# Experts of 56 slots with gathers for four pairs, gates by comparison, and a delta-net convolution that reads PSUM

## The chip, the cores and the metric

One program runs on one core of a Trainium2 chip. The metric is the device time of one execution in microseconds (us). A core has five engines that run side by side, each with its own instruction queue: TensorE (PE, matrix products, with a separate path PEld that loads the stationary operand), VectorE (DVE), ScalarE (ACT), GpSimd (POOL), and SyncE (SP), which here issues the DMAs. TensorE writes its results to PSUM, eight banks of 512 float32 columns on 128 partitions; everything else lies in SBUF.

## The reference

The input is 512 tokens of 1024 features. A first block has two layers (forgetting attention, then retention, each with a memory attention beside it). The second block has one layer: a mixer (a short convolution path and a gated delta net), then a mixture of experts, then a norm. The change touches the second block only. In short:

```
qkv  = silu(causal_dwconv(concat(q, k, v), conv_w))        # four taps along the tokens
q    = q * rsqrt(sum(q*q) + eps) * 128**-0.5 ; k likewise  # per head and token
y_a  = rms_norm(b * causal_dwconv(c * h, conv_a_w))        # three taps
...
group = argmax(h @ router_group_w)                         # 4 groups
two experts of the group's 8 by softmax, gate = group_prob * p / sum(p)
out[token] += gate * (silu(x @ w_gate[e]) * (x @ w_up[e])) @ w_down[e]
```

There are 32 experts and 512 x 2 = 1024 assignments of tokens to experts. Each expert has three float32 matrices of 2 MiB. With the inputs that are timed, the reference's router gives an expert between 19 and 41 assignments.

## The kernel before

Products in full float32 precision are made from two rounded halves (`wh`/`wl` of a weight, `hH`/`hL` of an activation), three products each, accumulated in an `acc` bank; four `acc` banks go round.

**Mixer.** `dn` walks a fixed list of pieces, `DN_ORDER`: f (a delta-net head's projections, convolutions and triangular inverse, up to the first yield of `dn_head`), s (the same head's scan over four chunks of tokens), z (an output gate), a (a quarter of the short convolution). The order of instructions on each engine inside this is chosen by the framework's scheduler, from dependencies and its own costs; PE then executes its queue strictly in that order. A projection is 24 matmuls into one `acc` bank. `conv` (L1186) handles its result: ACT copies the bank to a padded tile `cpad` (L1259), DVE scales it by the first tap (L1195) and adds three shifted taps (L1197) into `cy`. ACT makes tanh (L1261), DVE the silu `cs` (L1263), PE transposes `cs`, ACT squares the result (L1271), DVE sums the squares (L1272), and a reciprocal root of them scales Kh or Qh. The `acc` bank is free when ACT's copy is done.

**Experts.** Expert `e` owns 64 slots (`CAP`). `route` finds for each assignment its slot number `dest`; `build_S` (L1656, L1657) makes a 0/1 matrix `S3` of tokens by slots; `gather_T` multiplies the token features (`xH` and `xL`, L230 through `mm`) by it, which gives `mhT`, features by slots. One such gather serves a "quad": two pairs of experts, 4 x 64 = 256 slots, 64 matmuls of 256 columns. Experts are taken in 16 pairs. Per pair: `gate_up` of expert 0 and 1 (64 rows each, gate and up side by side, `pg`), `gu_out` (ACT scales by the slot's gate `us`), `act_T` (four PE transposes, then tanh and two DVE steps into `h`), `down` (`pd`), `y_out` (splits `pd` into `yh`, `yl`) and, a pair later, `combine` (16 matmuls with the 0/1 matrices `ST`, results added to `x` by DVE, L1852). `gates` (L1744 to L1755) gets `us` by four small matmuls of `gxs` with `S3` and eight tiny DVE steps. In this part PE's order is the order in which the code is written (`self.pe = self.ordered(...)`); DVE's and ACT's is the scheduler's.

**Weights.** Each expert's matrices come as six tiles of 1 MiB (1.0486 MB), in order of use, through a ring of 12 + 6 = 18 buffers (`wtile`, `NWA` + `NWB`). SP issues the DMA of a tile (L1767, L1812) when the matmuls that read the buffer's last content are done. 32 experts make 192 tiles.

Assignments beyond an expert's slots would go through `overflow`, a loop whose count comes from `spill`; with at most 41 to an expert it runs zero times.

Of the kernel before, what the change touches and what calls it, by code (L numbers as in the profile page):

```python
# [35 lines left out]
CAP = 64  # L36
NPAIR = NE // 2
SLOTS = NE * CAP
MAXOV = 16
# [3 lines left out]
NWB = 6  # L43
# [11 lines left out]
CM = ["ones", "iota", "ustrict", "eend", "pcol"]  # L55
# [8 lines left out]
def constants():  # L64
# [4 lines left out]
    c["ones"] = np.ones((P, P))  # L69
# [23 lines left out]
    c["pcol"] = np.stack([i, (i + CAP) % P], 1) - P  # L93
# [30 lines left out]
class Model:  # L124
# [689 lines left out]
    def out_router(self, W, heads):  # L814
# [13 lines left out]
        cm = self.rtp.tile([P, sum(self.off[k][1] for k in CM)], F32, tag="cm", name="cm")  # L828
        nc.sync.dma_start(cm, A["cm"])
        iota = self.const(cm, "iota")  # L830
        self.io3 = rp.tile([P, 2, CAP], F32, tag="io3", name="io3")
        V.tensor_copy(self.io3.rearrange("p a n -> p (a n)"), iota)
# [4 lines left out]
        V.tensor_copy(self.onesb, self.const(cm, "ones"))  # L837
        V.tensor_copy(self.ustb, self.const(cm, "ustrict"))
        V.tensor_copy(self.eend, self.const(cm, "eend"))
        V.tensor_scalar(out=self.e64b, in0=self.eend[0:1, :], scalar1=float(-CAP), scalar2=None, op0=ALU.add)  # L840
        self.pcol = rp.tile([P, 2, NPAIR], F32, tag="pcol", name="pcol")
        ends = self.eend.rearrange("p (n e) -> p n e", e=2)[:, None, :NPAIR, 1]
        nc.gpsimd.tensor_tensor(self.pcol, ends.to_broadcast([P, 2, NPAIR]),
                                self.const(cm, "pcol")[:, :, None].to_broadcast([P, 2, NPAIR]), op=ALU.add)
# [341 lines left out]
    def conv(self, wk, src, width, wv):  # L1186

        nc = self.nc
        V = nc.vector
        pad = width - 1  # L1190
        cp = wk.tile([P, S + 3], F32, tag="cpad", bufs=1, name="cpad")
        V.memset(cp[:, :pad], 0.0)
        src(cp[:, pad:pad + S])
        y = wk.tile([P, S], F32, tag="cy", name="cy")
        V.tensor_scalar(out=y, in0=cp[:, 0:S], scalar1=wv(0), scalar2=None, op0=ALU.mult)  # L1195
        for j in range(1, width):
            V.scalar_tensor_tensor(out=y, in0=cp[:, j:j + S], scalar=wv(j), in1=y, op0=ALU.mult, op1=ALU.add)  # L1197
        return y

    def short_conv(self, wk, ct, Wr, C):  # L1200
# [3 lines left out]
        for i in (2, 0, 1):  # L1204
# [4 lines left out]
        y = self.conv(wk, lambda d: V.tensor_tensor(d, pss[1], c, op=ALU.mult), 3,  # L1209
                      lambda j: aw[:, j * 4 + ct:j * 4 + ct + 1])  # L1210
# [18 lines left out]
    def dn_head(self, wk, h, Wr, C, sc, pre):  # L1229
# [23 lines left out]
        for n, (nm, c0) in enumerate(DNC):  # L1253
# [5 lines left out]
            y = self.conv(wk, lambda d: SC.activation(d, ps, AF.Copy), 4, lambda j: cw[:, j * 12 + ci:j * 12 + ci + 1])  # L1259
# [11 lines left out]
            SC.activation(sq, v4(pt), AF.Square)  # L1271
            V.tensor_reduce(ss[:, n * NT:(n + 1) * NT], sq, axis=AX.X, op=ALU.add)  # L1272
# [142 lines left out]
    def moe(self, psd):  # L1415
# [9 lines left out]
        io3 = self.io3  # L1425
        et = mc.tile([P, NPAIR, 1], F32, tag="et", name="et")
        blks = []
        quads = [dict(base=float(q * 2 * P), io=io3, n=2 * P) for q in range(NPAIR // 2)]
        for p in range(NPAIR):
            w = {}  # L1430
            for j in range(2):
                for n, src in (("g", "w_gate_2"), ("u", "w_up_2"), ("d", "w_down_2")):
                    w[n, j] = A[src][0, 2 * p + j]
            nc.gpsimd.tensor_scalar(out=et[:, p, :], in0=self.hm64[:, 1:2], scalar1=float(2 * p), scalar2=None, op0=ALU.add)
            blks.append(dict(pair=p, quad=quads[p // 2], cols=slice(p % 2 * P, (p % 2 + 1) * P), w=w, n=2,
                             e=et[:, p, :], cut=p == NPAIR - 1))
# [10 lines left out]
        self.gather_T(quads[0], True)  # L1447
# [3 lines left out]
        for p in range(nb):  # L1451
            more = p + 1 < nb

            def sums():
                if p:
                    self.combine(blks[p - 1], [(t, n) for n in range(2) for t in range(NT)])
                self.slots(blks[p])
                if more and p % 2:
                    self.build_S(quads[p // 2 + 1])
                if not p:  # L1460
                    ov.extend(self.spill(mc))
# [10 lines left out]
            if more:  # L1472
                if not p:
                    self.act_T(blks[0], 0)
                if p % 2:
                    self.gather_T(quads[p // 2 + 1])
                self.gates(blks[p + 1])
                self.down(blks[p], 0)
                self.act_T(blks[p], 1)
# [15 lines left out]
        self.overflow(mc, wk, io3, gb, ot, *ov)  # L1495

    def route(self, mc):
# [30 lines left out]
        iota = self.io3[:, 0, :]  # L1528
# [66 lines left out]
        G.tensor_tensor(self.gxs[:, :, 4:8], gx, self.gxs[:, :, 0:4].bitcast(F32), op=ALU.subtract)  # L1595

    def spill(self, mc):
# [11 lines left out]
        for m in range(2, 8):  # L1609
# [8 lines left out]
        for i in range(MAXOV):  # L1618
            cmp = sc[:, (8 + i % 2) * NE:(9 + i % 2) * NE]
# [18 lines left out]
    def build_S(self, blk):  # L1638
# [3 lines left out]
        S3 = wk.tile([P, NT, 2 * P], F32R, tag="S3", name="S3")  # L1642
        iof = blk["io"].rearrange("p a n -> p (a n)")
        ds = []
        for n in range(blk["n"] // P):
            dest = blk["dest"]
            if n or not isinstance(blk["base"], float) or blk["base"]:
                db = wk.tile([P, 2 * NT], F32, tag=f"db{n}", name="db")
                V.tensor_scalar(out=db, in0=dest, scalar1=blk["base"] + n * P if n else blk["base"], scalar2=None,
                                op0=ALU.subtract)  # L1650
                dest = db
            ds.append(dest)
        for t in range(NT):
# [7 lines left out]
    def gather_T(self, blk, first=False):  # L1661
# [4 lines left out]
        hT = blk["hT"] = wk.tile([P, KD, 2 * P], F32, tag="mhT", name="mhT")  # L1666
        pss = {}

        def mms(k, t, start):
            if k // 2 not in pss:  # L1670
                pss[k // 2] = self.att()
            o = pss[k // 2][:, k % 2 * 2 * P:k % 2 * 2 * P + n]
            for c, part in enumerate(self.xs):
                self.mm(o, part[:, t, k, :], S3[:, t, :n], start and c == 0,
                        t == NT - 1 and c == 1 and (not first or k % 2 == 1))

        def put(b):
            pv = pss[b].rearrange("p (k n) -> p k n", k=2)[:, :, :n]
            o = hT[:, 2 * b:2 * b + 2, :n]
            if b % 2:  # L1680
                nc.vector.tensor_tensor(o, pv, self.gv[:, 2 * b:2 * b + 2, None].to_broadcast([P, 2, n]), op=ALU.mult)
            else:
                for k in range(2):
                    nc.scalar.activation(o[:, k, :], pv[:, k, :], AF.Copy, scale=self.gv[:, 2 * b + k:2 * b + k + 1])

        if first:
            for t in range(NT):
                for k in range(KD):
                    mms(k, t, t == 0 and k % 2 == 0)
                    if t == NT - 1 and k % 2:  # L1690
                        put(k // 2)
        else:
            for k in range(KD):
                for t in range(NT):
                    mms(k, t, t == 0)
                if k % 2:
                    put(k // 2)
# [286 lines left out]
```

## Time and profile before

| | us |
|---|---|
| median of 3 runs | 1773.61 (1772.92 to 1774.19) |
| the profiled execution | 1773.5 |
| its span in the profile | 1771.7 |
| PE busy | 1724.4 (97%) |
| DVE busy | 1007.2 (57%) |
| ACT busy | 590.6 (33%) |

In the span the mixer takes about 965 to 1206 us, its output projection with the router until about 1251, the experts' loop from 1258 to about 1748, and the final norm the rest. An engine's busy time says how full it is; whether it sets the pace is read from what it waits for.

### The profile page before, as it was taken

Reading aid. Unit: us, or ns where it says so; the run is one execution under the profiler, and the core shown is the slowest. Engines: PE = TensorE matmul, PEld = TensorE weight load, DVE = VectorE, ACT = ScalarE, POOL = GpSimd, SP = SyncE. Lnnn points to the kernel's source line nnn. Section 1 sums busy time; section 2 is a strip of 40 time slices with the busy share of each in tenths; the row PEclk is TensorE's granted clock in tenths of the full one; section 3 lists DMA queues with packets and bytes.
Section 4 is the critical chain, followed back from the end, with each engine's and each line's share of the span. In section 5 each row is a group of like instructions: output and inputs, shape, how many; then the busy total and the mean of one; then the engine's idle time right before and its main releaser. Section 6 shows DMA issues by size and latency. Waiting matters only on the chain.

```text
span 1771.7 us, 24714 instructions
## 1 busy us (share of the span) xinstructions
PE 1724.4 (97%) x9410; PEld 1255.9 (71%) x9410; DVE 1007.2 (57%) x2660; ACT 590.6 (33%) x1173; POOL 96.6 (5%) x143
## 2 busy tenths in 40 slices
PE   8999999999999999999999999999999999999996
PEld 7888888878888888888888777778644445354443
DVE  7655564563757555454657978875545435453534
ACT  7643333433536232222446433334211111111112
POOL 0000000000000110111011000010200000000001
PEclk9999999999999999999999999999999999999998
DMA  8633233233223322223213342326799999999981
GB/s 260 175 96 90 81 93 95 73 86 96 69 92 99 92 85 82 84 75 103 76 48 81 91 111 62 85 69 265 301 418 418 410 409 420 407 407 407 420 321 49
DMA packets 199276, 318.82 MB, mean 180 GB/s; under 512 B 18789, under 2 KB 159590, under 8 KB 174450
## 3 DMA queue, kind: packets, MB, share of 16 engines
q1 hardware_dynamic: 199154, 317.21, 50.6%
q8 instruction: 75, 1.23, 0.3%
q14 instruction: 47, 0.39, 0.1%
HBM read 312.16 MB, written 5.01 MB: 179 GB/s over the span
## 4 chain that ended last, share of the span: by engine, by line
PE 89%; DVE 6%; ACT 2%; DMA 2%; issue 1%; SPq 0%; POOL 0%; POOLq 0%; ACTq 0%; DVEq 0%
PE acc L143 50%; PE pg L230 13%; PE att L143 8%; PE att L230 7%; PE pd L230 6%; PE trp L148 3%; PE trp L230 1%; PE trp L143 1%; DVE wl L205 1%; ACT wh L204 1%; DMA raw<-in_w_mem_kv_dram 1%; DVE cy L1197 1%; PE att L148 0%; ACT hH L243 0%; DMA kvf<-kvd 0%
## 5 line engine op out<-in xcount | busy, mean ns | idle before, releaser
L205 DVE TENSOR_TENSOR wl<-raw,wh 128x1024 fp32r<-128x1024 f32 x184 | 225.8, 1227 | 189.8 <-ACT wh L204 179.8
L143 PE MATMUL acc<-hH,wh 128*128 128x512 f32 (+1 forms) x760 | 297.3, 392 | 5.4 <-DVE sz L578 3.1
L143 PE MATMUL acc<-hL,wh 128*128 128x512 f32 (+1 forms) x760 | 299.1, 394 | 0.0
L143 PE MATMUL acc<-hH,wl 128*128 128x512 f32 (+1 forms) x760 | 298.0, 392 | 0.0
L204 ACT ACTIVATE wh<-raw 128x1024 fp32r<-128x1024 f32 x184 | 194.6, 1059 | 276.8 <-PE acc L143 262.2
L230 PE MATMUL pg<-mw,mhT 128*64 128x512 f32 x1024 | 230.3, 597 | 0.0
L143 PEld LDWEIGHTS acc<-hH,wh 128*128 128x128 f32 x760 | 143.7, 190 | 31.4 <-DVE sz L578 3.3
L143 PEld LDWEIGHTS acc<-hL,wh 128*128 128x128 f32 x760 | 144.0, 189 | 25.4
L143 PEld LDWEIGHTS acc<-hH,wl 128*128 128x128 f32 x760 | 144.0, 189 | 25.4 <-issue 1.0
L230 PEld LDWEIGHTS pg<-mw,mhT 128*64 128x64 f32 x1024 | 69.3, 137 | 129.8 <-issue 129.6
L143 PE MATMUL acc<-wh,hL 128*128 128x256 f32 (+1 forms) x384 | 129.5, 338 | 0.4 <-DVE hL L247 0.4
L143 PE MATMUL acc<-wh,hH 128*128 128x256 f32 (+1 forms) x384 | 129.3, 337 | 0.1
L143 PE MATMUL acc<-wl,hH 128*128 128x256 f32 (+1 forms) x384 | 129.3, 337 | 0.0
L143 PE MATMUL acc<-wh,oh 128*128 128x512 f32 x320 | 127.1, 397 | 1.4 <-ACT oh L243 1.4
L143 PE MATMUL acc<-wl,oh 128*128 128x512 f32 x320 | 126.4, 395 | 0.0
L143 PE MATMUL acc<-wh,ol 128*128 128x512 f32 x320 | 126.2, 395 | 0.0
L230 PE MATMUL pd<-mw,h 128*64 128x512 f32 (+1 forms) x544 | 116.7, 571 | 3.0 <-DVE h L1803 3.0
L1784 ACT ACTIVATE gu<-pg,gt 128x512 f32<-128x512 f32 x32 | 22.0, 687 | 266.7 <-PE pg L230 252.9
L1843 DVE TENSOR_TENSOR yl<-pd,yh 128x512 fp32r<-128x512 f32 x30 | 19.3, 687 | 137.0 <-ACT yh L1842 137.0
L1852 DVE TENSOR_TENSOR x<-att,x 128x512 f32<-128x512 f32 x120 | 73.1, 683 | 31.6 <-PE att L230 31.6
L230 PEld LDWEIGHTS pd<-mw,h 128*64 128x64 f32 x544 | 37.4, 137 | 66.3 <-issue 60.9
L143 PEld LDWEIGHTS acc<-wh,hH 128*128 128x128 f32 x384 | 73.0, 190 | 8.3 <-ACT hH L243 0.8
(567 smaller groups left out, 2863.3 us busy)
## 6 DMA issues: line engine op xcount, KB each, us to landing
mw<-in_w_gate_dram SPq DMA_DIRECT2D x64, 1024.0 KB
mw<-in_w_up_dram SPq DMA_DIRECT2D x64, 1024.0 KB
mw<-in_w_down_dram SPq DMA_DIRECT2D x62, 1024.0 KB
raw<-in_fox_w_in_dram SPq DMA_DIRECT2D x56, 512.0 KB
raw<-in_w_out_dram SPq DMA_DIRECT2D x40, 512.0 KB
raw<-in_w_in_dram SPq DMA_DIRECT2D x28, 512.0 KB
raw<-in_ret_w_in_dram SPq DMA_DIRECT2D x20, 512.0 KB
raw<-in_w_mem_kv_dram SPq DMA_DIRECT2D x16, 512.0 KB
```

The costliest lines, as they stand in the source:

```text
L143: self.pe.matmul(o, l, r, start=start, stop=stop)
L148: self.pe.transpose(o, i, self.ident[b:b + n, b:b + n])
L204: nc.scalar.activation(h, raw, AF.Copy)
L205: nc.vector.tensor_tensor(l, raw, h.bitcast(F32), op=ALU.subtract)
L230: ins = getattr(eng, name)(*a, **k)
L1197: V.scalar_tensor_tensor(out=y, in0=cp[:, j:j + S], scalar=wv(j), in1=y, op0=ALU.mult, op1=ALU.add)
L1784: nc.scalar.activation(gu, pg.rearrange("p (n k) -> p k n", k=4), AF.Copy, scale=blk["us"][:, j:j + 1])
L1843: V.tensor_tensor(l, pd, h.bitcast(F32), op=ALU.subtract)
L1852: self.nc.vector.tensor_tensor(xv, ps, xv, op=ALU.add)
```

## The change

1. `CAP` goes from 64 to 56. A gather then serves four pairs ("oct"): 8 x 56 = 448 slots, 64 matmuls of 448 columns, four gathers in all where there were eight. The halves of 64 rows stay (`RT`): an expert reads 64 columns of `mhT`, its 56 and 8 of a neighbour, whose gate is zero.
2. `mhT` and `S3` grow for that, and the ring of weight tiles goes from 18 to 16 (`NWB` 6 to 4).
3. `gates` compares the slots' numbers with the token rows `rows` on DVE, multiplies by the token's gate `grow` and sums along the tokens, four steps of 512 columns per pair; PE's four matmuls go. `grow` is made once, in `slot_rows`, by 16 matmuls of half width.
4. `conv` starts with ACT's scaled copy of the last tap into `cy`; DVE adds three taps straight from the `acc` bank. `cpad`, the DVE scaling and the memset go.
5. The squares are summed by ACT, four pieces of 128 columns with an accumulator, in place of one piece of 512 and DVE's reduction.
6. Some constants come by DMA in place of copies; `spill` is called after the first `down`.

```diff
-CAP = 64
+CAP = 56
+RT = 64
+OCT = 8 * CAP
...
-NWB = 6
+NWB = 4
...
-    def conv(self, wk, src, width, wv):
+    def conv(self, wk, x, width, wv):
...
-        cp = wk.tile([P, S + 3], F32, tag="cpad", bufs=1, name="cpad")
-        V.memset(cp[:, :pad], 0.0)
-        src(cp[:, pad:pad + S])
         y = wk.tile([P, S], F32, tag="cy", name="cy")
-        V.tensor_scalar(out=y, in0=cp[:, 0:S], scalar1=wv(0), scalar2=None, op0=ALU.mult)
-        for j in range(1, width):
-            V.scalar_tensor_tensor(out=y, in0=cp[:, j:j + S], scalar=wv(j), in1=y, op0=ALU.mult, op1=ALU.add)
+        nc.scalar.activation(y, x, AF.Copy, scale=wv(width - 1))
+        for d in range(1, width):
+            nc.vector.scalar_tensor_tensor(out=y[:, d:], in0=x[:, :S - d], scalar=wv(width - 1 - d), in1=y[:, d:],
+                                           op0=ALU.mult, op1=ALU.add)
...
-            y = self.conv(wk, lambda d: SC.activation(d, ps, AF.Copy), 4, lambda j: cw[:, j * 12 + ci:j * 12 + ci + 1])
+            y = self.conv(wk, ps, 4, lambda j: cw[:, j * 12 + ci:j * 12 + ci + 1])
...
-            SC.activation(sq, v4(pt), AF.Square)
-            V.tensor_reduce(ss[:, n * NT:(n + 1) * NT], sq, axis=AX.X, op=ALU.add)
+            for t in range(NT):
+                SC.activation(sq[:, t, :], v4(pt)[:, t, :], AF.Square, accum_out=ss[:, n * NT + t:n * NT + t + 1])
...
-        quads = [dict(base=float(q * 2 * P), io=io3, n=2 * P) for q in range(NPAIR // 2)]
+        octs = [dict(base=float(q * OCT), n=OCT) for q in range(NPAIR // 4)]
...
-                if more and p % 2:
-                    self.build_S(quads[p // 2 + 1])
-                if not p:
-                    ov.extend(self.spill(mc))
+                if more and p % 4 == 3:
+                    self.build_S(octs[p // 4 + 1])
...
-                if p % 2:
-                    self.gather_T(quads[p // 2 + 1])
+                if p % 4 == 3:
+                    self.gather_T(octs[p // 4 + 1])
...
+        self.grow = self.wk.tile([P, 2, S], F32, tag="grow", name="grow")
+        for i in range(2):
+            ps = self.att()
+            for t in range(NT):
+                for h in range(2):
+                    self.mm(ps[h * RT:(h + 1) * RT, t * P:(t + 1) * P],
+                            self.gr[:, t, i, h:h + 1].to_broadcast([P, RT]), self.ident, True, True)
+            self.nc.scalar.activation(self.grow[:, i, :], ps, AF.Copy)
...
     def gates(self, blk):
+        wk, V = self.wk, self.nc.vector
+        a = wk.tile([P, 2, 2], F32, tag="ga", bufs=2, name="ga")
+        for j in range(2):
+            for i in range(2):
+                junk = wk.tile([P, S], BF16, tag="gj", name="gj")
+                V.scalar_tensor_tensor(out=junk, in0=self.rows[:, i, :], scalar=self.ucol[:, j, blk["pair"]:blk["pair"] + 1],
+                                       in1=self.grow[:, i, :], op0=ALU.is_equal, op1=ALU.mult,
+                                       accum_out=a[:, i, j:j + 1])
+        us = wk.tile([P, 2], F32, tag="us", bufs=2, name="us")
+        V.tensor_tensor(us, a[:, 0, :], a[:, 1, :], op=ALU.add)
...
-                    self.mm(pg[i * CAP:(i + 1) * CAP, :], hT[:, kk, j * CAP:(j + 1) * CAP], wt[i][:, k, :],
+                    self.mm(pg[i * RT:(i + 1) * RT, :], hT[:, kk, c:c + RT], wt[i][:, k, :],
```

How the change moves instructions is seen at three places. First PE, from the end of the first gather (`att<-S`) into the first pair's `gate_up` (`pg`); `dest` and `gr` are the slot and gate columns that `slot_rows` spreads, `gxs` the old gates' operand, `ohb` belongs to `spill`. Before, then now:

```order
L230 MATMUL att<-S_12027,xL 128x256
L230 MATMUL att<-ident,dest 128x128 x8
L230 MATMUL pg<-mw,mhT 64x512 x16
L230 MATMUL trp<-gxs,S_12027 128x8 x4
L230 MATMUL pg<-mw,mhT 64x512 x8
L230 LDWEIGHTS rt
L230 MATMUL att<-ohb,rt 128x32
```

```order
L236 MATMUL att<-S_11985,xL 128x448
L236 MATMUL att<-ident,dest 128x128 x8
L236 MATMUL att<-ident,gr 64x128 x16
L236 MATMUL pg<-mw,mhT 64x512 x32
L236 MATMUL trp<-ident,gu 128x128 x4
L236 MATMUL pd_12278<-mw,h_12263 64x512
L236 MATMUL pd_12279<-mw,h_12263 64x512
```

The two short groups of `gxs` and `ohb` leave the middle of `pg`, 16 half-wide matmuls of `gr` stand in front of it, and `pd` follows `pg` with only the transposes between.

Second DVE, at the same time: the rows that stand just in front of the first pair's two `h` steps, on which the first `pd` waits (`S` is the 0/1 matrix of the next gather, `gj` a gate step, `ebt` part of `spill`). Before, then now:

```order
L1633 TENSOR_TENSOR sc<-sc 128x256
L1621 TENSOR_REDUCE ebt<-sc 128x1 x2
L1635 TENSOR_REDUCE dest_12320<-sc 128x8
L1620 TENSOR_SCALAR sc<-sc 128x32 x2
L1802 SCALAR_TENSOR_TENSOR h_12341<-h_12341,trp 128x256
L1621 TENSOR_REDUCE ebt<-sc 128x1 x2
L1803 SCALAR_TENSOR_TENSOR h_12341<-h_12341,trp 128x256
```

```order
L1663 TENSOR_SCALAR S_12785<-ioh,db 128x224
L1749 SCALAR_TENSOR_TENSOR gj,ga<-rows,pcol,grow 128x512
L1664 SCALAR_TENSOR_TENSOR S_12785<-ioh,db,S_12785 128x224
L1749 SCALAR_TENSOR_TENSOR gj,ga<-rows,pcol,grow 128x512
L1663 TENSOR_SCALAR S_12785<-ioh,db 128x224
L1749 SCALAR_TENSOR_TENSOR gj,ga<-rows,pcol,grow 128x512
L1664 SCALAR_TENSOR_TENSOR S_12785<-ioh,db,S_12785 128x224
L1753 TENSOR_TENSOR us<-ga 128x2
L1749 SCALAR_TENSOR_TENSOR gj,ga<-rows,pcol,grow 128x512
L1822 SCALAR_TENSOR_TENSOR h_12263<-h_12263,trp 128x256
L1749 SCALAR_TENSOR_TENSOR gj,ga<-rows,pcol,grow 128x512
L1823 SCALAR_TENSOR_TENSOR h_12263<-h_12263,trp 128x256
```

Before, small steps of `spill` stand there; now gate steps of the first four pairs and the next `S` do, 16 `gj` rows ahead of the first `h` in all.

Third DVE, at the start of the mixer: the convolution of the first head's k and the steps around it (`wl` is the low half of the next weight). Before, then now:

```order
L205 TENSOR_TENSOR wl<-raw,wh 128x1024
L1195 TENSOR_SCALAR cy<-cpad,vecs 128x512
L1197 SCALAR_TENSOR_TENSOR cy<-cpad,vecs,cy 128x512
L205 TENSOR_TENSOR wl<-raw,wh 128x1024
L1100 TENSOR_SCALAR beta<-beta 128x16
L1102 TENSOR_TENSOR sx<-trp,dtb 128x16
L1101 TENSOR_SCALAR hb<-beta 128x16
L1197 SCALAR_TENSOR_TENSOR cy<-cpad,vecs,cy 128x512
```

```order
L211 TENSOR_TENSOR wl<-raw,wh 128x1024
L1201 SCALAR_TENSOR_TENSOR cy<-acc,vecs,cy 128x511
L211 TENSOR_TENSOR wl<-raw,wh 128x1024
L1201 SCALAR_TENSOR_TENSOR cy<-acc,vecs,cy 128x510
L1109 TENSOR_SCALAR beta<-beta 128x16
L1111 TENSOR_TENSOR sx<-trp,dtb 128x16
L1110 TENSOR_SCALAR hb<-beta 128x16
L1201 SCALAR_TENSOR_TENSOR cy<-acc,vecs,cy 128x509
```

The scaling of `cpad` is gone, and the three taps that are left read the `acc` bank itself.

## Rows read from the trace of the kernel before

**Rows 1.** The page: busy us of the engines; GB/s in 40 slices of the span.

```profile
PE 1724.4 (97%) x9410; PEld 1255.9 (71%) x9410; DVE 1007.2 (57%) x2660; ACT 590.6 (33%) x1173; POOL 96.6 (5%) x143
GB/s 260 175 96 90 81 93 95 73 86 96 69 92 99 92 85 82 84 75 103 76 48 81 91 111 62 85 69 265 301 418 418 410 409 420 407 407 407 420 321 49
```

**Rows 2.** Chain of waits: start us, us, engine and line, instructions.

```profile
1224.46 14.18 PE acc L143 x62
...
1311.50 7.74 PE att L230 x64
1319.24 0.34 PE trp L230 x4
...
1345.93 0.54 PE trp L230 x4
...
1372.82 7.74 PE att L230 x64
...
1744.39 3.60 PE pd L230 x32
```

**Rows 3.** Waits of PE, 1290 to 1715: us in total, times, longest.

```profile
PEld att L230 <- DVE ST L1716: 5.7, 7, 0.8
```

**Rows 4.** Waits of the DMA queue on SP, 1190 to 1771: likewise.

```profile
SPq L1767 <- PE pg L230: 245.5, 55, 22.6
```

**Rows 5.** Stretches: busy us (x) of PE, PEld, DVE, ACT, POOL; PEclk, DMA, GB/s.

```profile
1320.00:1330.00 10.00, 10.00 (x50) 3.48 (x48) 2.40 (x13) 0.38 (x1) 0.00 (x0) 1.00 0.99 392
...
1360.00:1370.00 10.00, 10.00 (x46) 4.78 (x44) 6.08 (x11) 1.36 (x3) 0.00 (x0) 1.00 1.02 423
```

**Rows 6.** Timeline of PE at the loop's start: start us, us, what.

```profile
1258.02 0.36 PE L230 MATMUL att<-S,xH 128*128 128x256 f32 x1 [0.53 <-DVE S L1657]
...
1265.63 1.95 PE L230 MATMUL att<-ident,dest 128*128 128x128 f32 x16
1267.51 7.09 PE L230 MATMUL pg<-mw,mhT 128*64 128x512 f32 x32
...
1285.09 3.65 PE L230 MATMUL pd<-mw,h 128*64 128x512 f32 x16 [1.66 <-DVE h L1803]
```

**Rows 7.** Groups by form, 1300 to 1700: busy us, mean ns, idle before.

```profile
L1716 DVE SCALAR_TENSOR_TENSOR ST<-rows,pcol,ST 128x512 fp32r<-128x512 uint16 x26 | 18.4, 752 | 0.0
L1657 DVE SCALAR_TENSOR_TENSOR S<-io,db,S 128x128 fp32r<-128x128 f32 x48 | 15.2, 346 | 0.1
L1656 DVE TENSOR_SCALAR S<-io,db 128x128 fp32r<-128x128 f32 x48 | 12.3, 280 | 0.0
L1715 DVE TENSOR_SCALAR ST<-rows,pcol 128x512 fp32r<-128x512 uint16 x26 | 11.4, 482 | 0.0
L1803 DVE SCALAR_TENSOR_TENSOR h<-h,trp 128x256 f32<-128x256 f32 x26 | 10.9, 420 | 0.8
```

**Rows 8.** Groups by form in the mixer, 965 to 1206.

```profile
L1197 DVE SCALAR_TENSOR_TENSOR cy<-cpad,vecs,cy 128x512 f32<-128x512 f32 x44 | 32.7, 744 | 0.2
L1195 DVE TENSOR_SCALAR cy<-cpad,vecs 128x512 f32<-128x512 f32 x16 | 7.7, 481 | 0.6 <-issue 0.3
L1272 DVE TENSOR_REDUCE dss<-dtmp 128x4 f32<-128x512 f32 x8 | 5.4, 678 | 2.6 <-ACT dtmp L1271 2.6
L1226 DVE SCALAR_TENSOR_TENSOR ot<-trp,vecs,cy 128x512 f32<-128x512 f32 x4 | 3.0, 751 | 0.9 <-PE trp L148 0.8
...
L1404 ACT ACTIVATION_READ_ACCUMULATOR dtmp<-Y 128x1 f32 x16 | 3.0, 187 | 0.0
```

**Rows 9.** Stretches of the mixer, columns as in rows 5.

```profile
965.00:1025.00 60.00, 56.25 (x298) 45.64 (x297) 52.50 (x154) 29.16 (x47) 3.47 (x2) 1.00 0.34 89
1025.00:1205.00 180.00, 172.29 (x1115) 132.58 (x1114) 140.81 (x480) 66.05 (x155) 8.69 (x23) 0.98 0.32 82
```

**Rows 10.** Timelines of ACT, PE and DVE around one convolution.

```profile
992.56 0.58 ACT L1259 ACTIVATE cpad<-acc 128x512 f32<-128x512 f32 x1
...
999.66 0.48 PE L143 MATMUL acc<-hH,wh 128*128 128x512 f32 x1
...
1003.34 0.74 DVE L1197 SCALAR_TENSOR_TENSOR cy<-cpad,vecs,cy 128x512 f32<-128x512 f32 x1
```

More of the change, by code (lines that the diff above doesn't have):

```diff
@@ L92, in constants @@
     c["eend"] = np.broadcast_to(np.tile(CAP * (np.arange(NE) + 1.0), NT)[None, :], (P, NT * NE))
-    c["pcol"] = np.stack([i, (i + CAP) % P], 1) - P
+    e = np.arange(NE)[None, :]
+    row = i[:, None] % RT - np.where(e % 8 == 7, RT - CAP, 0)
+    ec = np.where((row >= 0) & (row < CAP), e * CAP + row, -1).reshape(P, NPAIR, 2)
+    up = i[:, None] >= RT
+    c["pcol"] = np.concatenate([np.where(up, ec[:, :, 1 - n], ec[:, :, n]) for n in range(2)], 1)
+    c["ucol"] = np.concatenate([ec[:, :, n] for n in range(2)], 1)
     c["uincl"] = (i[:, None] <= i[None, :]).astype(float)
@@ L836, in out_router @@
         self.e64b = rp.tile([1, P], BF16, tag="e64b", name="e64b")
-        V.tensor_copy(self.onesb, self.const(cm, "ones"))
+        V.memset(self.onesb, 1.0)
         V.tensor_copy(self.ustb, self.const(cm, "ustrict"))
-        V.tensor_copy(self.eend, self.const(cm, "eend"))
+        o = self.off["eend"][0]
+        nc.sync.dma_start(self.eend, A["cm"][:, o:o + P])
         V.tensor_scalar(out=self.e64b, in0=self.eend[0:1, :], scalar1=float(-CAP), scalar2=None, op0=ALU.add)
[L841 to L844, printed above, removed]
+        pc = rp.tile([P, 2, 2, NPAIR], F32, tag="pcol", name="pcol")
+        nc.sync.dma_start(pc.rearrange("p u a n -> p (u a n)"), A["cm"][:, o + P:o + P + 4 * NPAIR])
+        self.pcol, self.ucol = pc[:, 0], pc[:, 1]
         xH = rp.tile([P, NT, KD, P], F32R, tag="xH", name="xH")
@@ L1665, in gather_T, with mms, put @@
         n, S3 = blk["n"], blk["S3"]
-        hT = blk["hT"] = wk.tile([P, KD, 2 * P], F32, tag="mhT", name="mhT")
+        hT = blk["hT"] = wk.tile([P, KD, OCT], F32, tag="mhT", name="mhT")
         pss = {}
[L1669 to L1672, printed above, removed]
+        def mms(k, t):
+            if k not in pss:
+                pss[k] = self.att()
             for c, part in enumerate(self.xs):
[L1674 to L1681, printed above, removed]
-            else:
-                for k in range(2):
-                    nc.scalar.activation(o[:, k, :], pv[:, k, :], AF.Copy, scale=self.gv[:, 2 * b + k:2 * b + k + 1])
+                self.mm(pss[k][:, :n], part[:, t, k, :], S3[:, t, :n], t == 0 and c == 0, t == NT - 1 and c == 1)
+        def put(k):
+            if k % 2:
+                nc.vector.tensor_scalar(out=hT[:, k, :n], in0=pss[k][:, :n], scalar1=self.gv[:, k:k + 1], scalar2=None,
+                                        op0=ALU.mult)
+            else:
+                nc.scalar.activation(hT[:, k, :n], pss[k][:, :n], AF.Copy, scale=self.gv[:, k:k + 1])
         if first:
[L1687 to L1691, printed above, removed]
+            for k0 in (0, 4):
+                for t in range(NT):
+                    for k in range(k0, k0 + 4):
+                        mms(k, t)
+                        if t == NT - 1:
+                            put(k)
         else:
```

148 lines of the change are left out of this document (75 added, 73 removed).

## The prediction

> **What bounds the kernel now.** I read the page first: PE is busy for 97% of the span, DVE for 57%, ACT for 33% [rows 1]. A share does not say where an end is set, so the chain of waits came next: from 1224 us to the end it is PE almost without a break, and two pairs of experts lie between one gather at 1311.50 and the next at 1372.82, 61.32 us apart [rows 2]. The waits of PE in 1290 to 1715 agree: of what has a name, the largest sum is 5.7 us for seven waits on `ST`, and no row names a DMA [rows 3]. The waits of the DMA queue say the same from the other side: SP waited 55 times, 245.5 us, for PE to finish with a buffer [rows 4]. So in the loop what leaves PE's queue leaves the time, as long as the weights keep up. They have little to spare: 24 tiles of 1.0486 MB in 61.32 us are 410 GB/s, and a stretch with no pause in the queue moved 423 GB/s, one around a gather 392 [rows 5]. In the mixer PE was idle for 3.75 of 60 us and then 7.7 of 180 us [rows 9], so it gives at most 11.5 us to whoever removes all its waits.
>
> **The change part by part.** Time is measured against the profiled execution, 1773.5 us: a span of 1771.7 us and 1.8 us around it. The median of the runs, 1773.61, is the same within 0.1 us, and nothing is added for that.
>
> *Gathers.* A gather of 256 columns took 7.74 us for 64 matmuls [rows 2], 0.121 us each; matmuls of 512 columns took 14.18/62 = 0.229 us [rows 2]. No row has 448 columns. The straight line between the two gives 0.202 us, 12.9 us a gather; the bounds are the 512 price (14.6 us) and 7.74 us, which would be no cost for width at all and which I do not believe, since 512 columns cost nearly twice 256. Of eight gathers four remain. The seven later ones were 7 x 7.74 = 54.2 us on PE's chain and become three, 3 x 12.9 = 38.7: **-15.5** (between -10 and -31).
>
> *The gates on PE.* Each pair's four small matmuls of `gxs` stand in the chain with 0.34 or 0.54 us [rows 2]. Fourteen of them come after the first `pd`: 7 x 0.34 + 7 x 0.54 = **-6.2**. In their place DVE gets four 512-column steps per pair, about 2.8 us where eight tiny ones were; beside a PE period of some 30 us per pair, and with gates of a pair made pairs ahead of need, that is hidden. If it were not, DVE would be late with `ST` or `h` and rows 3 would show more.
>
> *The loop's start.* Here nothing overlaps, since everything waits for the first gather. Before, PE went: gather 1258.02 to 1265.63, `dest` 1.95, `pg` from 1267.51, first `pd` at 1285.09, 1.66 us of it a wait on DVE's `h` [rows 6].
> - The first gather: 12.9 for 7.6, **+5.3**. Its `S3` pieces are wider, 224 columns for 128: the first matmul starts **+0.3** later (a few steps at the difference of rows 7's prices).
> - The 16 matmuls of `gr`: the order's 8 `dest` matmuls cost 1.95 (the trace counts two passes for each), 0.24 each. Half-width `pg` matmuls at 7.09/32 = 0.222 us [rows 6] cost what full-width `acc` ones of as many columns do, so half the width saves nothing: 16 x 0.24 = **+3.9** (at half price 1.95).
> - From `pg` to the first `pd`: 17.6 us before. PE's and ACT's own path is now 32 `pg`, four transposes and the tanh, about 16.7 us, but DVE has a queue in front of `h`. The order shows 16 `gj` rows ahead of the first `h`, and 16 steps of the next `S`. The second `grow` lies in SBUF about 0.7 us after `pg` starts (an ACT copy of a bank took 0.58 [rows 10]). Behind that point stand some 15 `gj`, priced like the `ST` step of the same shape, 18.4/26 = 0.708 us [rows 7]: 10.6; one `ST` step 0.7; 13 `S` steps, between the 128-column and 512-column rows at 0.30 and 0.41 us [rows 7]: 4.7; three small sums 0.3; 15 reads of an accumulator, unseen on DVE, 0.1 each as I take it (nothing, or ACT's 0.187 [rows 8]): 1.5; then two `h` steps of 0.42 with a `gj` between: 1.6. Together 0.7 + 19.4 = 20.1 us, so the first `pd` comes **+2.5** later (at the price of 0.438 of the cheaper `ST` step DVE is ready before PE, and it is -0.9; with dear accumulators +3.9). What is late here is `h`, in place of the last row of [rows 6].
> - `spill`'s small matmuls move behind the first `pd`, into PE's chain: **+0.2**.
>
> Start +12.2, later -21.7: **-9.5**.
>
> *The ring.* Two tiles fewer are in flight. First `pg` starts about 9.5 us later, its first 16 matmuls (half of 7.09) release the first two buffers at about 1280.6; the remaining 176 tiles at 420 GB/s, 2.497 us each, and 2 us that I allow for the landing bring the last one in at about 1722. The last 32 `pd` start at 1744.39 before [rows 2], 27.3 us before the end of the span, so now at about 1735: 13 us of slack. Four pairs take 122.6 - 15.5 + 12.9 - 4 x 0.44 = 118.3 us by PE and 48 x 2.497 = 119.9 by the weights; the lead shrinks by under 2 us each time, and holds. Price: nothing.
>
> The Trainium skill says otherwise: its page "DMA: Bandwidth & Descriptors", section "Specifications", puts the limit of the HBM side at about 358 GB/s for each core. By that a tile takes 2.93 us, the same sum ends at 1827 us, and the kernel before would have been bound by its weights too, at 562 us for 192 tiles. The trace disagrees: the queue moved 423 GB/s over 10 us [rows 5] and PE waited for no DMA [rows 3].
>
> *The convolution.* DVE loses 16 scalings of 0.48 us and eight reductions of 0.68 [rows 8], 13.1 us, besides the memsets; ACT's copy stays a pass of 512 columns with a scale, its squares become four pieces with an accumulator read of 0.187 each, some 1.4 us per square and about 11 us in all. ACT is busy for 29.16 of 60 us, then 66 of 180 [rows 9], and has room. The three taps now read PSUM: a step like them from PSUM took 751 ns, from SBUF 744 [rows 8], so 44 x 7 ns = 0.3 us. PE's matmuls here are the same in number and PE is within 11.5 us of full. DVE is close to full in the first stretch (52.5 of 60 us), so some of PE's 3.75 us of idle time may come back; against it stands a bank that is held longer. I take **0**, between -6 (half of PE's idle time) and +13 (rival C).
>
> On the same step the skill's page "VectorE: DVE Perf Modes", section "Rules for kernel authors", advises a copy from PSUM to SBUF first where many operations follow. By it three taps from PSUM should cost DVE something; the two rows differ by 1%, so here the copy bought DVE no time and the rule changes 0.3 us.
>
> Sum: 1773.5 - 9.5 = **1764.0 us**.
>
> **Rivals.**
> *B, the weights become the bound.* PE now needs 48 tiles in 118.3 us, 425 GB/s, which no row before holds for long. By the sum above the end is 1280.6 + 176 t + 2 + 27.3 + 1.8 for a tile time t; it passes 1764 at t = 2.572, 408 GB/s. At 403 GB/s (2.6 us) it is 1769; at the 392 of the gather's stretch 1782. For it: 410 was the mean. Against: the mean has SP's waits for PE in it, and the low stretches lie at gathers, where no buffer comes free. Chance 0.10.
>
> *C, slower: the convolution holds its bank.* Before, ACT freed the first head's k bank at 992.56 + 0.58 = 993.14; the third tap ended at 1003.34 + 0.74 = 1004.08, and the fourth group after it, counted by 24 matmuls from the row at 999.66 [rows 10], wants the bank near 1001.0. If the taps stay where they were, PE stands there 3.1 us, about 4.4 in all for a head's three convolutions, and 13 for the three heads that have others behind them: 1777. It decides if DVE's relief by then, some 3.5 us, does not bring the third tap forward by as much. For it: DVE does these taps late, behind the splits of weights. Against: the relief is as large as the delay. Chance 0.09.
>
> *D, the mixer gains.* DVE's relief reaches PE, and half of the idle time goes: 1758. For it 52.5 of 60 us on DVE; against, most of PE's waits there are short and of several causes. Chance 0.13.
>
> That the change does not do what it says is not a case: the order shows the 448-column gathers, and `trp<-gxs` gone.
>
> **How the numbers follow.** The forecast's case A has 0.68; its own range is 1758 to 1770 (the bounds of the gather width and of DVE's queue, which do not add up on one side). To hold 8 in 10 over all cases the range goes from 1755, D with a cheap start, to 1774, most of B and the mild part of C. A measurement of this kernel cannot tell less than 0.2%, 3.5 us, from no change. Faster than 1770: A nearly whole (0.63), D (0.13), the mild part of B (0.05): 0.81. Within: the edge of A and the middle of B and C: 0.11. Slower: the rest of C, B at its worst: 0.08.
>
> **What would show it.** Gather rows of 64 matmuls with about 12.9 us, four of them, and four pairs in about 118.3 us (122.6 before); the first `pd` behind its `pg` by some 20 us, waiting on `h`; the first `gj` rows at 0.7 to 0.9 us; no `trp<-gxs`; SP still waiting for PE in the loop and PE for no DMA; the mixer from 965 us to the first gather as long as before. C would be a wait of `acc` on the `cy` taps, D a shorter mixer, B waits of `pg` or `pd` on `mw`. The forecast is wrong if a 448-column matmul costs as much as one of 512, if PE stands for weights in the loop, or if the mixer moves by more than 4 us.

## The result and the profile after

The changed kernel takes 1754.24 us (median of 6 runs, 1751.23 to 1762.39), the kernel before 1773.9 us (6 runs beside them): a ratio of 0.9891, 95% interval 0.9875 to 0.9907. The forecast was 1764.0 with a range from 1755 to 1774: right in direction, but the gain is twice the one that was worked out, and the time lies 0.8 us below the range. The profiled execution has a span of 1753.8 us, 17.9 less than before.

The page of the changed kernel, busy us of the engines and GB/s in 40 slices; they answer to [rows 1]:

```profile
PE 1708.9 (97%) x9122; PEld 1238.9 (71%) x9122; DVE 1012.4 (58%) x2523; ACT 595.8 (34%) x1219; POOL 91.5 (5%) x130
GB/s 255 184 97 89 80 85 96 84 85 91 66 92 97 73 86 106 86 73 73 111 61 55 104 100 74 93 65 305 127 384 420 414 419 420 419 420 420 419 420 123
```

Shares say little again: PE is at 97% as before. The two traces have to be laid against each other at places that both have. Four suffice: the last `few` matmul (the mixer's beginning), the last projection matmul, the first gather, the first `pd`.

| stretch | before | after | difference |
|---|---|---|---|
| start to the last `few` matmul | 964.7 | 965.3 | +0.6 |
| to the last projection matmul (the mixer and its output projection) | 281.85 | 271.07 | -10.8 |
| to the first gather (router) | 11.4 | 14.2 | +2.8 |
| first gather to first `pd` | 27.1 | 37.3 | +10.3 |
| first `pd` to the end | 486.6 | 465.9 | -20.7 |

The last three lines together are what the forecast called the gathers, the gates and the loop's start: -7.6 us, where it said -9.5. The mixer, which it left at 0, gave -10.8.

**The mixer.** One stretch in the view by windows: busy us (and instructions) of PE, PEld, DVE, ACT and POOL, then the granted clock, the DMA share and GB/s. First the kernel before, then the changed one:

```profile
964.74:1246.59 281.85, 270.39 (x1632) 212.92 (x1631) 212.74 (x669) 114.42 (x226) 13.71 (x26) 0.99 0.40 120
```

```profile
965.30:1236.37 271.07, 266.52 (x1631) 211.02 (x1630) 201.64 (x631) 121.91 (x286) 8.11 (x9) 1.00 0.42 129
```

The matmuls are the same (one record apart), yet PE is busy 3.9 us less: they ran faster. The rest, 11.46 - 4.55 = 6.9 us, is idle time of PE that went. DVE does 11 us less work, ACT 7.5 more. The waits of PE from 965 to 1230 (us in total, times, longest), before and after (`sz` is an output gate, `cs` the silu behind a convolution, `KT` the transposed k, `XX` a tile of the triangular inverse):

```profile
PE acc L143 <- DVE sz L578: 3.1, 1, 3.1
PE acc L143 <- ACT cpad L1259: 2.2, 1, 2.2
PE att L143 <- DMA XX<-ldx: 1.9, 1, 1.9
```

```profile
PE att L154 <- DVE cs L1268: 1.4, 2, 0.9
PE att L149 <- DMA XX<-ldx: 1.0, 1, 1.0
PE att L149 <- ACT KT L1301: 0.6, 1, 0.6
```

Before, PE stood twice for an `acc` bank that was emptied late, by DVE's `sz` once and once by ACT's copy to `cpad`, the padded tile; now no `acc` waits. Each of the two waits was followed by slow matmuls. Windows of the kernel before, around them:

```profile
1072.00:1074.00 2.00, 0.48 (x3) 0.06 (x1) 2.00 (x6) 1.49 (x2) 0.00 (x0) 1.00 0.00 0
1074.00:1080.00 6.00, 5.27 (x18) 4.28 (x19) 4.77 (x16) 1.28 (x3) 0.00 (x0) 0.72 0.33 87
...
1134.00:1137.00 3.00, 0.00 (x0) 0.00 (x0) 3.00 (x9) 2.15 (x5) 0.98 (x1) 0.91 0.00 0
1137.00:1140.00 3.00, 3.00 (x7) 2.41 (x8) 3.00 (x8) 1.06 (x2) 0.00 (x0) 0.52 0.14 31
```

PE idles, then the granted clock is at its lower level, 1.2 of 2.4 GHz, for some microseconds. By an estimate from these windows 6 x 0.28 + 3 x 0.48 = 3.1 us are lost there, most of the 3.9. DVE is busy in every microsecond of both idle stretches: PE stood behind DVE's queue. A reduction of the squares is part of it; ahead of the second wait it stood 1.44 us for ACT's square, and everything behind it in the queue stood too, `sz` among it:

```profile
1131.51 0.69 DVE L1272 TENSOR_REDUCE dss<-dtmp 128x4 f32<-128x512 f32 x1 [1.44 <-ACT dtmp L1271]
...
1136.27 0.68 DVE L578 SCALAR_TENSOR_TENSOR sz<-th,acc 128x512 f32<-128x512 f32 x1
```

**The router.** PE and DVE of the changed kernel (start us, us, what, and in brackets the idle time in front and what ended it):

```profile
1250.56 0.71 PE L236 MATMUL att<-S,xH 128*128 128x448 f32 x1 [3.34 <-DVE S L1664]
```

```profile
1246.06 0.42 DVE L1562 TENSOR_REDUCE dest<-sc 128x8 f32<-128x256 f32 x1
1249.07 0.09 DVE L1619 MEMSET sc<- 128x32 f32 x1 [2.59 <-ACT sc L1584]
1249.07 0.13 DVE L1654 TENSOR_SCALAR db<-dest 128x8 f32<-128x8 f32 x1
1249.12 0.33 DVE L1663 TENSOR_SCALAR S<-ioh,dest 128x224 fp32r<-128x224 uint16 x1
```

`S3` could have begun when `dest` was there, at 1246.5. In front of it in DVE's queue stands a tiny memset that belongs to `spill`. `spill` now keeps its numbers in a part of `sc` that ACT still reads for the gates, so the memset waits 2.59 us for ACT, and all behind it with it. No piece of the forecast had this. In this execution the clock made it dearer; windows of the changed kernel over the first gather:

```profile
1250.50:1256.00 5.50, 5.44 (x15) 4.86 (x16) 3.96 (x16) 0.00 (x0) 1.23 (x8) 0.50 0.00 0
1256.00:1266.50 10.50, 10.50 (x52) 9.61 (x51) 2.03 (x3) 2.15 (x4) 0.34 (x3) 0.97 0.00 1
```

**The loop's start and the loop.** PE's timeline, which answers to [rows 6], and the chain of waits, which answers to [rows 2]:

```profile
1266.46 1.95 PE L236 MATMUL att<-ident,dest 128*128 128x128 f32 x16
1268.34 1.97 PE L236 MATMUL att<-ident,gr 128*64 128x128 f32 x32
1270.13 13.90 PE L236 MATMUL pg<-mw,mhT 128*64 128x512 f32 x64
...
1287.91 1.12 PE L236 MATMUL pd<-mw,h 128*64 128x512 f32 x2 [3.29 <-DVE h L1823]
```

```profile
1250.56 16.07 PE att L236 x64
1287.91 5.03 PE pd L236 x16
...
1368.20 13.28 PE att L236 x64
...
1486.44 13.28 PE att L236 x64
```

The first gather costs 16.07 us with its start at half clock, the later ones 13.28. From one later gather to the next, over four pairs, it is 1486.44 - 1368.20 = 118.2 us; the forecast had 118.3. In 1290 to 1715 no wait of PE itself names a DMA. Its loader PEld, which [rows 3] was about, now names the weights `mw` for 14 gaps of at most 0.4 us, 4.0 us in all; PE did not stand for them, its only wait there is one of 1.4 us on `h`. SP still stands for PE; its largest wait, which answers to [rows 4]:

```profile
SPq L1787 <- PE pg L236: 132.2, 28, 35.9
```

The gate steps by form in 1255 to 1300:

```profile
L1749 DVE SCALAR_TENSOR_TENSOR gj<-rows,pcol,grow 128x512 bf16<-128x512 uint16 x20 | 15.0, 749 | 0.0
...
L1749 DVE DVE_READ_ACCUMULATOR gj<-rows,pcol,grow 128x1 f32 x20 | 1.7, 86 | 0.0
```

### The profile page after: what moved, and what is told of

Same layout as the page of the kernel before. It is cut to its first block, busy times and chain, and to the rows that moved or that the text cites. A ratio compares the mean times of both kernels' runs of the same rounds, so it can differ in the third digit from the quotient of the medians.

```text
span 1753.8 us, 24034 instructions
## 1 busy us (share of the span) xinstructions
PE 1708.9 (97%) x9122; PEld 1238.9 (71%) x9122; DVE 1012.4 (58%) x2523; ACT 595.8 (34%) x1219; POOL 91.5 (5%) x130
## 4 chain that ended last, share of the span: by engine, by line
PE 88%; DVE 6%; ACT 2%; DMA 1%; issue 1%; POOL 0%; SPq 0%; POOLq 0%; ACTq 0%; DVEq 0%
PE acc L149 50%; PE pg L236 12%; PE att L149 7%; PE att L236 7%; PE pd L236 6%; PE trp L154 3%; PE trp L236 1%; DVE wl L211 1%; PE trp L149 1%; DVE gj L1749 1%; DVE cy L1201 0%; ACT wh L210 0%; DMA kvf<-kvd 0%; PE att L154 0%; ACT hH L249 0%
## 5 line engine op out<-in xcount | busy, mean ns | idle before, releaser
L1804 ACT ACTIVATE gu<-pg,us 128x512 f32<-128x512 f32 x32 | 22.0, 687 | 265.7 <-PE pg L236 265.7
```

The lines of the kernel that those rows point to most:

```text
L1804: nc.scalar.activation(gu, pg.rearrange("p (n k) -> p k n", k=4), AF.Copy, scale=blk["us"][:, j:j + 1])
```

## Experiments

Three theories stood for the mixer's gain: B, the single padded tile held the bank; D, DVE's load counts; O, the gain is in the order that the scheduler made of PE's queue, which nearly every edit changes. A letter with "theory" is one of the experiments; the forecast's rivals B, C and D are named as such. "Stretch" below is the one of the table above, from the last `few` matmul to the last projection matmul, in the profiled execution (281.85 us before, 271.07 after). Ratios are to the kernel before.

**e1, parts 4 and 5 alone.** The kernel before with the new `conv` and the new squares, as in the diff of the change.

> The kernel before with parts 4 and 5 of the change alone (first tap on ScalarE, three taps from PSUM, squares summed on ScalarE); the experts as before. Theory M (the mixer gave what the forecast missed): about 10.5 us under the kernel before, near 1763; the stretch from 965 us to the output projection's 62 matmuls about 249 us long where it was 259.5, PE idle there under 5 us, and no stretch of 20 us under a granted clock of 0.99. Rival L (the gain belongs to the experts' part and the mixer only shifted): within 2 us of the kernel before.

Measured: 1766.64 us, 0.996 (0.9948 to 0.9973); stretch 272.93. Most of the mixer's gain is there without the experts' part, though the time is 3.6 us above the 1763 expected; rival L falls. In the stretch PE's and ACT's orders are those of the changed kernel row for row, DVE's but for four rows.

**e2, part 4 alone** (the squares stay on DVE).

```diff
-            y = self.conv(wk, lambda d: SC.activation(d, ps, AF.Copy), 4, ...)
+            y = self.conv(wk, ps, 4, ...)
```

> The kernel before with part 4 alone: the convolution reads PSUM after ScalarE's first tap, the squares are reduced on DVE as before. Theory B (the single padded tile held the bank: ScalarE's copy waited for the last tap of the convolution ahead, and PE for the copy): most of it, 7 to 10 us faster, and no wait of acc on ScalarE's copy near 1075 us. Theory D (DVE's total load is what counts, 7.7 us of scalings here against 5.4 of reductions): about 6 us. Theory O (only the order of PE's queue that the scheduler made of the whole change is lucky): anything, within 3 us of before or slower, since this order differs from both.

Measured: 1770.57 us, 0.9982 (0.9973 to 0.9991); stretch 278.09. Far less than theory B wanted. PE's longest wait in it, and the DVE steps in front:

```profile
1069.51 0.77 PE L143 MATMUL acc<-hH,wh 128*128 128x512 f32 x1 [4.52 <-DVE drt L175]
```

```profile
1066.46 0.68 DVE L1268 TENSOR_REDUCE dss<-dtmp 128x4 f32<-128x512 f32 x1
1067.06 0.74 DVE L1192 SCALAR_TENSOR_TENSOR cy<-acc,vecs,cy 128x511 f32<-128x511 f32 x1
...
1068.61 0.75 DVE L1192 SCALAR_TENSOR_TENSOR cy<-acc,vecs,cy 128x509 f32<-128x509 f32 x1
1069.28 0.15 DVE L175 TENSOR_TENSOR drt<-drr 128x4 f32<-128x4 f32 x1
```

The profile names a small `drt` step as the releaser, but that step reads no `acc`. The third tap ends at 1069.36, and PE starts 0.15 us later, as it started 0.15 us behind `S` at 1250.56 above. The view leaves out the numbers of the banks, so it is inferred that this tap's bank is the one. It is the forecast's rival C: the bank is held until the last tap has read it, and here PE pays 4.5 us. The two waits of before are not in its list of waits; this one is, and 1.7 us of `acc` on another step of DVE.

**e3, part 5 alone.**

```diff
-            SC.activation(sq, v4(pt), AF.Square)
-            V.tensor_reduce(ss[:, n * NT:(n + 1) * NT], sq, axis=AX.X, op=ALU.add)
+            for t in range(NT):
+                SC.activation(sq[:, t, :], v4(pt)[:, t, :], AF.Square, accum_out=ss[:, n * NT + t:n * NT + t + 1])
```

> The kernel before with part 5 alone: squares summed on ScalarE in four pieces, padded tile and four DVE steps as before. Theory B: 0 to 3 us faster, the wait of acc near 1075 us still there in some form. Theory D: about 4 us faster. Theory O: anything within 3 us, or slower.

Measured: 1764.22 us, 0.9952 (0.9939 to 0.9964); stretch 272.07. Part 5 alone brings all of the mixer's gain, more than B or D gave it. Eight reductions are 5.4 us of DVE [rows 8], and DVE stood 2.6 us in front of them for ACT's square. The edit is not the only difference, though: the scheduler gave 273 of the mixer's 1218 matmuls another place in PE's queue (for e1, 373).

**e4, two padded tiles.**

```diff
-        cp = wk.tile([P, S + 3], F32, tag="cpad", bufs=1, name="cpad")
+        cp = wk.tile([P, S + 3], F32, tag="cpad", bufs=2, name="cpad")
```

> The kernel before with two padded tiles in place of one, nothing else. Theory B: the 2.25 us wait of acc near 1075 us goes and with it the stretch at half clock behind it (about 1.8 us): 3 to 5 us faster; the other wait near 1137 us (acc on sz) stays. Theory D: no change, since DVE has the same work, within 1 us.

Measured: 1769.33 us, 0.9973 (0.9961 to 0.9985); stretch 277.20. As theory B said for its one wait: `acc` on `cpad` falls from 2.2 to 0.8 us, `acc` on `sz` stays at 3.1. Here too PE's order moved, by some 240 of the stretch's 1630 matmuls, so it is not shown that the gain of about 5 us is the tile's own.

**e5, the changed kernel with parts 4 and 5 undone.**

> The changed kernel with parts 4 and 5 undone (padded tile, four DVE steps, DVE reductions), the experts as changed. Theory M: about 10 us over the changed kernel, near 1764 where the changed kernel is 1754, and with the two waits of acc near 1075 and 1137 us back, each with a stretch at half clock. Rival L: like the changed kernel within 2 us. This is also the forecast's own sum, which left the mixer at 0: 1764.

Measured: 1765.41 us, 0.9947 (0.9928 to 0.9966); stretch 284.45, with the waits of `acc` on `sz` (3.1) and on `cpad` (2.2) back. The orders of PE, DVE and ACT in the stretch are those of before but for five rows of DVE. The experts' part alone is what the forecast's sum was about, and it lands 1.4 us from its 1764.0; how much of that is luck is said below. The wait on the memset is here too, but not the slow clock behind it:

```profile
1263.64 0.44 PE L236 MATMUL att<-S,xH 128*128 128x448 f32 x1 [3.34 <-DVE S L1668]
```

```profile
1263.60:1269.00 5.40, 5.36 (x27) 5.06 (x28) 3.95 (x16) 0.00 (x0) 1.14 (x7) 1.00 0.01 3
```

**e8 to e10, load and order apart.** PE's 1218 matmuls of the mixer are recorded as they are written and tied to a given order (`PE_SEQ`); DVE's and ACT's orders are the scheduler's. e10 is the kernel before in the PE order of e1.

```diff
+        self.pe = _Rec(nc.tensor)
...
+        got = self.pe.got
+        seq = [a + i for a, n in PE_SEQ for i in range(n)]
+        for a, b in zip(seq[1:], seq):
+            self.after(got[a], got[b])
```

> The kernel before, word for word, but PE's 1218 matmuls of the mixer are tied to the order that the scheduler made with the squares on ScalarE (the kernel of e3); the reductions stay on DVE. Theory O (the order of PE's queue gave the 10 us of e3): about 10 us faster than before, near 1764, and 272 us from the last `few` matmul to the last projection matmul, where before has 281.9. Theory D (DVE's shorter queue gave it): within 3 us of before or slower, PE waiting longer on what DVE makes.

> The kernel of e3 (squares on ScalarE, nothing else), with the mixer's PE order tied to that of the kernel before. Theory O: near the kernel before, within 3 us, and the waits of acc near 1075 and 1137 us back. Theory D: 6 to 10 us faster than before, those waits short.

> The kernel before with PE's mixer order tied to that of e1 (parts 4 and 5 of the change). Theory O: about 8 us faster, like e1. Theory D: within 3 us of before or slower.

| PE's order \ squares | on DVE | on ScalarE |
|---|---|---|
| of before | before, 1773.9 | e9: 1774.3, 1.0002 (0.9991 to 1.0013) |
| of e3 | e8: 1772.38, 0.9988 (0.9979 to 0.9996) | e3: 1764.22, 0.9952 (0.9939 to 0.9964) |

e10 is slower: 1779.78 us, 1.0034 (1.0022 to 1.0047). Both theories fall as they were put. The lighter DVE in the old order gives nothing, the new order with the heavy DVE 1.6 us, both together 10. In e9 PE waits at the two old places, each 0.3 to 0.7 us shorter, and longest at a new one, on `Qh` (its lines are shifted by the added code); its waits from 965 to 1230:

```profile
PE trp L140 <- DVE Qh L1315: 3.4, 2, 2.0
PE acc L140 <- DVE sz L611: 2.4, 1, 2.4
PE acc L140 <- ACT cpad L1299: 1.9, 1, 1.9
```

In e8, the new order with the heavy DVE, no wait on `acc` is left, but PE stands for other steps of DVE, and its stretch of 277.92 us holds 10.5 us of idle time:

```profile
PE trp L139 <- DVE cs L1302: 2.0, 3, 0.8
PE att L139 <- DVE cs L1302: 2.0, 2, 1.7
PE att L139 <- DVE drt L208: 1.7, 2, 1.1
```

Over the stretches of e9 and e3 the windows read (e9, then e3):

```profile
964.18:1248.67 284.49, 273.10 (x1631) 215.37 (x1630) 209.97 (x661) 118.63 (x282) 12.83 (x26) 0.98 0.39 119
```

```profile
964.58:1236.65 272.07, 267.26 (x1631) 210.46 (x1630) 207.28 (x661) 118.65 (x282) 13.46 (x26) 1.00 0.41 125
```

The same instructions on DVE and ACT, 11.4 us of idle time against 4.8, and a clock of 0.98 against 1.00. So the two long waits on the banks went with PE's order (e3 keeps one of 1.3 us on `sz`), and in these four kernels what DVE saved was worth something only together with it. What stays open is how much of it lies in the order of DVE's and ACT's own queues, which the scheduler made anew in each of these kernels: e9's DVE order differs from both that of before and that of e3. No run ties a kernel to its own order either, so what the tie itself costs is not known.

**e6, the memset behind the first `S3`.**

```diff
-        V.memset(ones, 1.0)
+        self.after(V.memset(ones, 1.0), self.S0)
```

> The changed kernel with one small memset of the later overflow count (128 x 32) ordered behind the first S3 instead of in front of it on DVE. Theory W (the first gather waits 3.34 us because DVE stands at that memset until ScalarE has read the same buffer, and PE's idle time then puts the gather's first 6 us at half clock): S3 starts 2.6 us earlier, PE idle before the first gather about 0.7 us, the first gather 13.3 us in place of 15.9: 5 to 5.5 us faster than the changed kernel. Rival V (only the wait goes, the clock falls for another reason): 2.6 us. Rival N (S3 waits for something else): 0.

Measured: 1751.44 us, 0.987 (0.9854 to 0.9886). In the trace the wait and the slow clock are both gone, as theory W said: PE waits 0.82 us and the first gather takes 13.06.

```profile
1247.83 0.44 PE L236 MATMUL att<-S,xH 128*128 128x448 f32 x1 [0.82 <-DVE S L1664]
```

The span is 5.6 us shorter than the changed kernel's, the median 2.8, near rival V's 2.6; the two intervals overlap. That the memset is what `S3` and PE waited for is shown. That the slow clock always follows is not: e5 has the same wait and a clock of 1.00 behind it.

**e7 and e12, the gates behind the first `h` as well.**

```diff
+                if hasattr(self, "h0"):
+                    self.after(o1, self.h0)
...
+                if blk["pair"]:
+                    self.after(g, self.h0)
```

(`o1` is a step of the next `S`, `g` a gate step, `h0` the first pair's first `h`.)

> The same, and the gate steps of pairs 1 to 3 and the next S3 ordered behind the first pair's h on DVE. If DVE's queue is what sets the first pd (the forecast's step of +2.5 us), the first pd follows its pg by about 16 us where the changed kernel has 17.8, 1.5 to 2 us faster than with the late memset alone; if PE and ScalarE set it, no difference. A loss would mean that a later gate or ST became late.

> The kernel of e7 unchanged, beside e11 on the same chip: near 1749, 5 us faster than the changed kernel's 1754.

Measured: 1749.17 us, 0.9857 (0.9839 to 0.9875), and again 1749.92, 0.9867 (0.9851 to 0.9884): the fastest version, 4 to 5 us under the changed kernel by the medians, though e12's interval overlaps the changed kernel's. The first `pd` comes 15.94 us behind its `pg` in place of 17.78 (17.77 in e6), at full clock:

```profile
1281.71 3.65 PE L236 MATMUL pd<-mw,h 128*64 128x512 f32 x16 [1.44 <-DVE h L1827]
```

So DVE's queue did set the first `pd`. Beyond e6 the median gained 2.3 us, within the intervals' overlap.

**e11, e7 with the old taps and the new squares.**

> The kernel of e7 with part 4 undone (padded tile, DVE scaling, taps from SBUF) and part 5 kept (squares on ScalarE). If part 5 gives the mixer's gain and part 4 nothing beside it, as e1 and e3 suggest (1766.6 and 1764.2), this runs like e7 within 2 us, or up to 2 us faster. If the two add up inside the whole change (after's mixer stretch 271.07 us, e3's 272.08), it is 1 us slower. A loss of over 4 us would mean that the taps from PSUM are what the changed experts' kernel lives on.

Measured: 1750.72 us, 0.9876 (0.986 to 0.9893), beside 1749.92 for e12 on the same chip; stretch 271.94 (e7: 271.84). Its stretch has the orders of e3 but for five rows of DVE. Part 4 is worth nothing that can be told beside part 5.

## Why the prediction was wrong

**The step that failed** is the convolution: "I take **0**", with bounds of -6 and +13. Measured -10.8 us (stretch), -10 by e3, and -10 (ratios) to -11 (medians) by the changed kernel against e5. Three things in its working were off.
- It priced the reductions as 5.4 us of DVE's busy time in a kernel where PE has the last word. They are more than that: a reduction that waits for ACT's square holds all that is queued behind it, as at 1131.51 above, where `sz` and with it an `acc` bank came later. That alone is not the gain, however: in e9 the reductions are gone, PE's order is that of before, and the two waits shrink only from 3.1 and 2.2 us to 2.4 and 1.9.
- It took PE's idle time, 11.5 us, for all that could be had. The granted clock from 1025 to 1205 is 0.98 in [rows 9]; that column was not read. By an estimate from it 0.02 x 180 = 3.6 us more could be had, and the windows above put most of it behind the same waits.
- It kept the order of before in mind ("if the taps stay where they were") for gain and loss alike. The orders that the scheduler made differ by 273 (e3) and 373 (e1) of PE's 1218 matmuls in the mixer, and e8, e9 and e3 show that 10 us hang on order and load together.

Rival D, with a chance of 0.13 and half the idle time as its price, had the outcome, at 6.9 us of idle time and 3.9 of clock; of its mechanism, DVE's relief reaching PE, the runs show only that it does so together with another order. Rival C came in e2, at 4.5 us. In e1 and the changed kernel, with the squares moved too, no wait on `acc` is left; whether the shorter DVE queue or PE's other order brought that about is not shown.

**The experts' part**, point by point. Later gathers -14.3 for -15.5: a 448-column matmul is 13.28/64 = 0.2075 us, the straight line said 0.202. Gates on PE: without its gathers a pair took (61.32 - 7.74)/2 = 26.79 us before and takes (118.24 - 13.28)/4 = 26.24, which is 0.55 less and not 0.44: over fourteen pairs -7.7 for -6.2. First gather +8.3 for +5.3: 5.5 at full clock, the rest is the slow clock behind the wait for the memset. `gr` +1.8 for +3.9: a pass with 64 stationary columns takes 1.97/32 = 0.06 us where one of 128 takes 1.95/16 = 0.12, so half a width does save half here. What set the price in the forecast, `pg` against `acc`, were matmuls of 512 columns, where the width of the stationary operand does not show. From `pg` to the first `pd` +0.2 for +2.5, though the mechanism is the one described: 16 `gj` of 0.749 us with an accumulator read of 0.086 stood before `h`, and PE waited 3.29 us on it. The first gate step began with `pg` (1270.11) and not 0.7 us behind it, and with their reads overlapping the steps took less than the prices added up to. The clock after that wait added 1.4 us (`pd` 5.03 for 3.65). The wait of 2.6 us on the memset was missed (first matmul +2.8 for +0.3; in e6, without it, +0.2): the forecast looked at the order of DVE at two places, and not in front of the first gather. These pieces sum to -7.5 us, beside -7.6 in the table; the +0.2 for `spill` was not read apart. So the forecast's -9.5 is near by luck in part: dear pieces (`gr`, the way to the first `pd`) and missed ones (the memset, the slow clock) cancel. In e5's trace, which has the memset's wait and no slow clock, the same three lines of the table give 14.2, 34.3 and 464.5 us, together 12.1 less than before.

The taps from PSUM cost no more than those from SBUF: 741 ns on average for 511 columns after, 744 for 512 before; [rows 8] had led to 751.

**The weights** did not become the bound: four pairs took 118.2 us, no wait of PE itself names a DMA, and the page shows 414 to 420 GB/s in each slice from 1315 to 1710 us. Rival B did not come, but there was less to spare than forecast. In SP's waits from 1190 us on, those for weight transfers sum to 97.8 us where they were 5.5, and the transfers end between 1715 and 1720, some 7 us ahead of the last 32 `pd` at 1726.6, where the forecast had 13. The limit of about 358 GB/s for each core, which the Trainium skill's page "DMA: Bandwidth & Descriptors", section "Specifications", gives, stands there as half of what a stack gives two cores. The forecast read it as the limit of one core that runs by itself, which these 414 to 420 GB/s contradict.

## What to carry to other kernels

An engine that empties another's buffers is to be priced by when it lets a buffer go, not by its busy time; look for steps in its queue that wait for a third engine. Where a scheduler orders the queues, a lighter load may pay only together with another order, as here, so an edit is to be tried in the scheduler's order and in the old one before its gain is put down to either. Read the clock beside the idle time: a wait of PE was often paid twice, once as idle time and once as slow matmuls behind it.

## What was not expected of the hardware

The clock's fall is not the same in every execution of one program. e12 is e7 unchanged; its windows over the stretch, e7 first:

```profile
965.71:1237.55 271.84, 266.49 (x1631) 210.96 (x1630) 201.55 (x631) 121.88 (x286) 8.11 (x9) 1.00 0.41 128
```

```profile
965.16:1242.39 277.23, 272.31 (x1631) 214.93 (x1630) 201.59 (x631) 121.82 (x286) 8.14 (x9) 0.98 0.41 126
```

The idle time is 5.35 and 4.92 us, PE's longest wait 1.4 and 1.5 us, at the same instruction (`att` on `XX`). Behind it the clock stayed up in e7 (1.00 in 1020 to 1040) and fell in e12, which cost 5.8 us of busy time:

```profile
1020.00:1040.00 20.00, 18.49 (x125) 13.77 (x124) 11.41 (x34) 3.90 (x6) 0.00 (x0) 0.75 0.52 124
```

The wait on the memset shows the same: half clock behind 3.34 us of idle time in the changed kernel, full clock behind as much in e5. The stretch of the changed kernel, with PE's and ACT's orders the same in all of them, took 271.07 to 272.93 us in four traces (the changed kernel, e1, e6, e7) and 277.23 in the fifth (e12); that of before took 281.85 and, in e5, 284.45. A single trace of this kernel is thus good to about 5 us where PE has such a wait, and that may be why the changed kernel's runs spread over 11 us; mechanisms are read from traces here, sizes from medians.
